# Start and end of a hybrid decoder layer: first weights by ScalarE's queue, one output block by ScalarE and an adding transfer, one load cut in two, one square moved

## The chip, the cores and the metric

The kernel runs on one core of one Trainium2 chip. The core has five engines that run beside each other, each with its own instruction queue in program order: TensorE (PE; its weight loads are PEld), VectorE (DVE), ScalarE (ACT), GpSimd (POOL) and SyncE (SP). SP, ACT and POOL can issue DMA transfers. The metric is the device time of one execution in microseconds (us), lower is better.

## The reference

One layer of a decoder trunk on 256 tokens, with 16 learned meta tokens ahead of them (L = 272), D = 2048, all in float32:

```
h = concat(meta, x)
u = rms_norm(h, g_pre_mix);  proj = u @ w_in
z_pool, v_conv, g_conv, gate_a, gate_b = split(proj)
y_a = causal_multiscale_pool(z_pool) @ w_pool_out
y_b = silu(layer_norm(depthwise_conv(v_conv * sigmoid(g_conv)))) @ w_conv_out
m = sigmoid(gate_a) * y_a + sigmoid(gate_b) * y_b
h = h + rms_norm(m @ w_o, g_post_mix)
f = square(relu(rms_norm(h, g_pre_mlp) @ w_up)) @ w_down
out = (h + rms_norm(f, g_post_mlp))[16:]
```

`rms_norm` divides each token's row by the root of the mean of its squares and multiplies by a gain per channel.

## The kernel before

**Exact products.** Each float32 operand is split into a high part (`hi`, a cast on ACT) and a low part (`lo = raw - hi`, a subtraction on DVE). A product is hi*hi + hi*lo + lo*hi, three matmuls (`mm3`) for each block of 128 channels. So every chunk of weights (1 MB, called `raw...`) passes through DMA, ACT (cast) and DVE (subtraction) before PE can use it.

**The first pass.** It computes 256 of the convolution's columns (`v_conv`) in two PSUM banks (`accs`, `acc_v`). Its weights are the chunks `raw_0` and `raw_1`, loaded in pieces. For each of the KD = 16 blocks of channels `x_tile(k)` turns the tokens (two PE transposes into `xt_k`) and splits them, with the gain `g_pre_mix`, into the high and low part of `u`; `pieces_to(k + 1)` splits the weights' piece; `mm3` then multiplies. The meta tokens come in by `meta_tiles` and four `meta_parts`. Token loads (`load_x`) stand between the weights' pieces in SP's queue (`X_BEHIND`). `keep_warm` issues transposes that nobody reads.

**The token norm comes late.** The factor 1/rms of a token is not applied to `u`. `sq_tile` squares and sums the tokens on ACT: eight squares of 128 x 512 for `x` and four of 16 x 512 for the meta tokens. Those for `x` whose turn comes within the first pass are issued there, on odd k from `SQUARES_FROM` = 5 on; `squares_left` puts all others into the plan (below). Behind the last square come `mean` (DVE, `tot`), `root` (ACT, `rs_q_in`) and `newton` (DVE: five small steps to `r_in`, then three diagonal tiles `v`). `rows_step` then multiplies the diagonals with ones on PE (L898), which spreads the factor over all partitions in bank `y0`; DVE copies it to `rb`, and every bank of the first passes is scaled by `rb` when DVE empties it.

**The second pass on.** The second pass's first megabyte is `raw_2` (chunk number `FIRST` = 2), split in four pieces that the first pass's last steps issue. Then come `raw_s0a` (two chunks), `raw_p0`, `raw_p1`, `raw_p2` and so on. From here the order is made by a plan: steps are listed with an engine, a cost, reads and writes (`plan.add`), PE's order is as listed, and `Plan.order` simulates the engines. An engine that becomes free in that simulation takes, among the steps that are ready by then, the one that is due first (L148), even if a more urgent one is about to become ready. The order found is issued as it stands; on the chip every engine keeps it and waits on semaphores.

**The end.** A second plan covers the last product. The output has two halves of 128 tokens (t = 0 and 1) and four column blocks of 512. `finish_down(t, cuts)` computes block by block on DVE `dst * r + h` (L2187; `norm3.r` is the last norm's factor, the `raw{rooms_h[t]}` rooms hold h, loaded from `kept` in DRAM) and issues the output's transfer. `half_done` handles the two last halves of a block for t = 1; the second one makes `r1`.

Of the kernel before, what the change touches and what calls it, by code (L numbers as in the profile page):

```python
# [12 lines left out]
AF = mybir.ActivationFunctionType  # L13
ALU = mybir.AluOpType
PSUM = bass.MemoryType.PSUM

P = 128
CK = 4
CW = 512
# [13 lines left out]
SQUARES_FROM = 5  # L33
# [177 lines left out]
def hybrid_block(ctx: ExitStack, tc: tile.TileContext, ins: dict, out: bass.AP):  # L211
    nc = tc.nc
    x = ins["x"][0]
    meta = ins["meta"]
    T, D = x.shape
    M = meta.shape[0]
    L = M + T
    NT = T // P
    KD = D // P
# [26 lines left out]
    def f32(ap):  # L246
        return ap.bitcast(F32)

    def acc_tile(name):
        return psA.tile([P, CW], F32, tag="acc", name=name)  # L250
# [44 lines left out]
    NB = D // CW  # L295
# [4 lines left out]
    FIRST = KD // HALF[0]  # L300
# [9 lines left out]
    opened = []  # L310
# [14 lines left out]
    def part_tile(tag, n):  # L325
        key = f"{tag}{n % 3}"
        room = ready.pop(key) if key in ready else part_room(key, f"{tag}_{n}")
        place = PLACES.get(n, (1, 1))[("hi", "lo").index(tag)]
        shift = (place - 1 - 3 * KEYS.index(key)) % 4 * LINE
        return room[:, shift:shift + CK * CW]  # L330

    def open_chunk():
        n, slot = at["n"], at["slot"]
        at["n"] += 1
        at["slot"] += 1
        if n >= UP:
            PLACES[slot] = (2, 1)
        src, (rows, width) = stream[n]
        raw = raws.tile([P, CK * CW], F32, tag="raw", name=f"raw_{n}")
        if n in spare:  # L340
            both = big.tile([P, 2, CK * CW], F32R, tag=spare[n], name=f"parts_{n}")
            hi, lo = both[:, 0, :], both[:, 1, :]
        else:
            hi, lo = part_tile("hi", slot), part_tile("lo", slot)
        raw, hi, lo = (t.rearrange("p (k c) -> p k c", k=rows) for t in (raw, hi, lo))
        pieces = rows if n < FIRST else 4 if n == FIRST else 1
        k = rows // pieces
        cuts = ((0, 1, 2, 4, 6, 8), (0, 2, 4, 6, 8))[n] if n < FIRST else (0, rows)
        for a_, b_ in zip(cuts, cuts[1:]):
            sl = slice(a_, b_)  # L350
            nc.sync.dma_start(raw[:, sl, :], src[:, sl, :])
            if (n, b_) in X_BEHIND:
                load_x(X_BEHIND[n, b_])

        def high(sl):
            nc.scalar.copy(hi[:, sl, :], raw[:, sl, :])

        def low(sl):
            nc.vector.tensor_sub(lo[:, sl, :], raw[:, sl, :], f32(hi[:, sl, :]))

        def piece(i):
            def f():
                sl = slice(i * k, (i + 1) * k)
                high(sl)
                low(sl)
            return f
        todo = [piece(i) for i in range(pieces)]
        if n in spare:
            todo = [lambda: high(slice(0, rows)), lambda: low(slice(0, rows))]
        opened.append((hi, lo, todo))  # L370
# [53 lines left out]
    def col(name, k):  # L424
        return vecs[:, cols[name] + k:cols[name] + k + 1]
# [4 lines left out]
    def load_x(b):  # L430
        sl = slice(b * X_COLS, (b + 1) * X_COLS)
        nc.sync.dma_start(x_in[:, :, sl], xv[:, :, sl])
# [20 lines left out]
    def keep_warm(n):  # L453
        for _ in range(n):
            nc.tensor.transpose(idle[:, :P], ident, ident)
# [30 lines left out]
    u = Tokens((K_FIRST, "um", 0), (KD - K_FIRST, "um8", 3 * LINE))  # L486

    def x_tile(k):
        pt = acc_tile(f"xt_{k}")
        sl = slice(k * P, (k + 1) * P)  # L490
        for t in range(NT):
            nc.tensor.transpose(pt[:, t * P:(t + 1) * P], x_in[:, t, sl], ident)
        at_ = slice(M, L)
        nc.scalar.activation(u[:, k, 0, at_], pt[:, :T], AF.Copy, scale=col("g_pre_mix", k))
        nc.vector.scalar_tensor_tensor(
            u[:, k, 1, at_], pt[:, :T], col("g_pre_mix", k), f32(u[:, k, 0, at_]),
            op0=ALU.mult, op1=ALU.subtract)
# [19 lines left out]
    def sq_tile(b, t):  # L517
        sl = slice(b * CW, (b + 1) * CW)
        junk = tmp.tile([P, CW], F32, tag="junk", bufs=1, name=f"sqx_{b}_{t}")
        src, n = (x_in[:, t, sl], P) if t < NT else (m_in[:, sl], M)  # L520
        nc.scalar.activation(junk[:n, :], src, AF.Square, accum_out=ssq[:n, t, b:b + 1])
# [12 lines left out]
    def mm3(acc, hi, lo, act, k, cs, first, last):  # L534


        off = act.shape[3] - acc.shape[1]
        for n, (w, a) in enumerate(((hi, 0), (hi, 1), (lo, 0))):
            nc.tensor.matmul(acc, w[:, k[0], cs], act[:, k[1], a, off:],  # L539
                             start=first and n == 0, stop=last and n == 2)  # L540
# [18 lines left out]
    def acc_tiles(name, n=CW // P):  # L559
        return [acc_tile(f"acc_{name}_{j}") for j in range(n)]  # L560
# [5 lines left out]
    def pieces_to(n):  # L566

        while first["split"] < min(n, FIRST * HALF[0]):
            c = first["split"] // HALF[0]
            opened[c][2].pop(0)()  # L570
            first["split"] += 1
# [4 lines left out]
    accs = [acc[:, :L] for acc in first_banks]  # L576
    squares = [(b, t) for b in range(XB) for t in range(NT)] + [(b, NT) for b in range(XB)]
    LEAD = 3
    TURNS = {0: (2, 3), 1: (), 2: (4, 5)}

    def turn_and_split(k):
        if k < KD:
            x_tile(k)
        pieces_to(k + 1)

    meta_parts.pop(0)()
    for k in range(2):
        turn_and_split(k)
    keep_warm(DUMMIES[1])
    for k in range(KD):  # L590
        for j, acc in enumerate(accs):
            mm3(acc, *opened[k // HALF[0]][:2], u, (k % HALF[0], k), slice(j * P, (j + 1) * P),
                k == 0, k == KD - 1)
        for n in TURNS.get(k, (k + LEAD,)):
            turn_and_split(n)
        if k < 3:
            meta_parts.pop(0)()
        if k >= SQUARES_FROM and k % 2 and k < KD - LEAD:
            sq_tile(*squares.pop(0))
        for _ in range((2, 1, 1)[k - KD + LEAD] if k >= KD - LEAD else 0):  # L600
            opened[FIRST][2].pop(0)()
# [13 lines left out]
    plan = LoadedPlan()  # L615
# [125 lines left out]
    n = 0  # L741
# [759 lines left out]
    norm3 = Norm("mlp")  # L1501
    ssq2 = const.tile([P, NT, NB], F32, name="ssq2")
    kept = dram.tile([P, NT, D], F32, name="kept")
# [155 lines left out]
    accs = acc_tiles("up00")  # L1659
# [51 lines left out]
    hi, lo = fetch()  # L1711
# [36 lines left out]
    ov = out[0].rearrange("(t p) d -> p t d", p=P)  # L1748

    plan = LoadedPlan()  # L1750
# [71 lines left out]
    def raw_in(room):  # L1822
        return room_of[room][:, :CK * CW]
# [289 lines left out]
    for j in range(4):  # L2113
        plan.add("PE", 1.36, last_of_first(j), reads=(f"hi{q0}", f"lo{q0}"),
                 writes=(f"x{j // 2}{j % 2}",))
    loads()
    for t in range(NT):
        plan.add("ACT", 0.92, lambda t=t: square_h1(t, NB - 1),
                 reads=[f"raw{r}" for r in H_ROOMS], writes=("junk", "ssq2"))
# [10 lines left out]
    for s, i in steps:  # L2130
        if s == "R":
            plan.add("PE", 0.9, rows2, reads=("diag2",), writes=("b",))
            plan.add("DVE", 0.4, lambda: nc.vector.tensor_copy(rb[:, :T], banks["b"][:, :T]),
                     reads=("b",), writes=("rb",))
# [39 lines left out]
    for t in range(NT):  # L2174
        add_bank(t, 2, f"x0{t}")
        for n in range(NB - 1):
# [2 lines left out]
        plan.add("DVE", 0.4, lambda t=t: norm3.start(t),  # L2179
                 reads=[f"ssq{t}{n}" for n in range(NB - 1)], writes=(f"v{t}",))  # L2180

    def finish_down(t, cuts, ahead=(), after=()):
        for n, (c0, c1) in enumerate(zip(cuts, cuts[1:])):
            dst = dst_of(t, c0, c1)

            def f(dst=dst, c0=c0, c1=c1, queue=(nc.sync, nc.scalar)[t * n % 2]):
                nc.vector.scalar_tensor_tensor(dst, dst, norm3.r[:, t],  # L2187
                                               raw_in(rooms_h[t])[:, c0:c1],
                                               op0=ALU.mult, op1=ALU.add)
                queue.dma_start(ov[:, t, c0:c1], dst)  # L2190
            plan.add("DVE", (c1 - c0 + 151) / 960 - 0.02, f,
                     reads=[f"out{t}{b}" for b in range(c0 // CW, (c1 - 1) // CW + 1)]
                     + [f"r{t}", f"raw{rooms_h[t]}", *after], writes=ahead)

    ends = [(m_, "X3"), (m_ + 1, "X4")]
    for w, s in ends:
        h = AT[s][0]
        plan.add("PE", 2.72, lambda w=w, h=h: down(banks["x10"], split_at[w], h, A1, False, h == 1),
                 reads=half_names(w) + act_names(h, A1), writes=("x10",), late=0.2)
    whole, name = total_of(0, NB - 1)  # L2200
    total = raw_in(room_s)[:, :CW]
    plan.add("DVE", 0.61, lambda: nc.vector.tensor_add(total, whole, banks["x10"]),
             reads=("x10", name), writes=(f"raw{room_s}",), late=0.1)
    plan.add("ACT", 0.92, lambda: square_of(total, norm3.ssq, 0, NB - 1), reads=(f"raw{room_s}",),
             writes=("junk", f"ssq0{NB - 1}"))
    plan.add("DVE", 0.69, lambda: nc.vector.tensor_mul(whole, total,
                                                       raw_in(room_g)[:, block(NB - 1)]),
             reads=(f"raw{room_s}", f"raw{room_g}"), writes=(f"out0{NB - 1}", name))
    plan.add("DVE", 1.3, lambda: norm3.finish(0), reads=("v0", f"ssq0{NB - 1}"), writes=("r0",))
    finish_down(0, (0, CW), ("first out",))  # L2210
    col_halves = [slice(h * HALF_CW, (h + 1) * HALF_CW) for h in range(2)]
    last_ssq = const.tile([P, 2], F32, name="last_ssq")
    for e, cs in enumerate(col_halves):
        for w, s in ends:
# [3 lines left out]
                reads=half_names(w) + act_names(h, A2), writes=("ab"[e],), late=0.2)  # L2218

        def half_done(e=e, cs=cs):  # L2220
# [9 lines left out]
            else:  # L2230
                for f in norm3.steps(1, last_ssq[:, 1:2]):
                    f()
        plan.add("DVE", (0.9, 2.3)[e], half_done,
                 reads=("ab"[e], "G3", "v1", ("first out", "next out")[e]),
                 writes=("junk", "v1", "G3", "out13") + (("r1",) if e else ()))
        if e == 0:
            finish_down(0, (CW, 2 * CW, 3 * CW), ("next out",))
    finish_down(0, (3 * CW, D), after=("r1",))
    finish_down(1, (0, 384, D // 2, D // 2 + CW, D - HALF_CW, D))
    plan.emit()  # L2240

# [24 lines left out]
```

## Time and profile before

| | us |
|---|---|
| median of 3 runs (lowest, highest) | 1180.18 (1179.68, 1180.21) |
| the profiled execution: its own time | 1180.13 |
| the profiled execution: span in the trace | 1178.3 |
| busy: PE, PEld | 1165.8, 1011.7 |
| busy: DVE, ACT, POOL | 1064.0, 707.3, 65.5 |

The trace's times count from the span's start. 1.83 us of the execution lie outside the span. Rows of a timeline give start, duration, engine, source line, operation, output and inputs, and in brackets the engine's idle time before the row with what ended it. "SPq" and "ACTq" are the queues' issue of a transfer. Matmuls are pipelined, so a row's duration is longer than the distance to the next.

### The profile page before, as it was taken

The page shows a single profiled execution, that of the slowest core. Times are in us where ns is not written, and L with a number is a line of the kernel's source. Part 1 is how long each engine was busy: PE and PEld are TensorE (multiplying, and loading weights), DVE is VectorE, ACT ScalarE, POOL GpSimd, SP SyncE. Part 2 cuts the span into 40 slices and gives each one's busy share as a digit, 9 for nine tenths or more (in the row PEclk, how much of TensorE's full clock was granted, in tenths as well). Part 3 has the DMA queues.
Part 4 walks back from the last instruction along what each step waited for, and adds up shares of the span by engine and source line. Part 5 has one row for each costly group of instructions (what it writes and reads, how often), then busy time and mean ns, then how long its engine had stood idle before and what let it go on. Part 6 is the DMA issues. An engine that isn't in the chain of part 4 may idle for free.

```text
span 1178.3 us, 15808 instructions
## 1 busy us (share of the span) xinstructions
PE 1165.8 (99%) x6301; PEld 1011.7 (86%) x6301; DVE 1064.0 (90%) x1156; ACT 707.3 (60%) x719; POOL 65.5 (6%) x68
## 2 busy tenths in 40 slices
PE   9999999999999999999999999999999999999996
PEld 8999998788888888898888888888888888888885
DVE  5899999999998998688998998998989989989857
ACT  6634455556478666575775666666656756656542
POOL 1000000000000000000101001000000010010000
PEclk9999999999999999999999999999999999999998
DMA  9955356789866799468999999999999999999941
GB/s 288 286 191 179 108 179 178 237 272 298 218 194 245 212 352 292 151 221 278 263 310 235 249 318 258 250 288 244 302 263 227 341 237 249 317 240 240 341 144 71
DMA packets 186977, 287.70 MB, mean 244 GB/s; under 512 B 4905, under 2 KB 94697, under 8 KB 186120
## 3 DMA queue, kind: packets, MB, share of 16 engines
q1 hardware_dynamic: 161960, 234.44, 58.2%
q0 software_dynamic: 24480, 51.67, 24.0%
q8 instruction: 49, 0.80, 0.3%
q10 hardware_dynamic: 464, 0.60, 0.1%
q14 instruction: 24, 0.20, 0.0%
HBM read 282.49 MB, written 4.19 MB: 243 GB/s over the span
## 4 chain that ended last, share of the span: by engine, by line
PE 95%; DMA 2%; DVE 2%; issue 0%; ACT 0%; DVEq 0%; POOL 0%; ACTq 0%; POOLq 0%
PE bank_u L544 18%; PE bank_k L1262 16%; PE acc_up L2005 13%; PE bank_u L550 9%; PE acc_v L1262 9%; PE bank_k L539 8%; PE bank_a L2005 7%; PE bank_b L2005 5%; PE acc_v L539 4%; PE acc_up L544 1%; DMA raw_k<-in_w_in_dram 1%; PE bank_u L2005 1%; DMA raw_p<-in_w_in_dram 1%; DVE lo L832 1%; PE acc_up L550 1%
## 5 line engine op out<-in xcount | busy, mean ns | idle before, releaser
L544 PE MATMUL bank_u<-m,hi 128*128 128x512 f32 x960 | 329.2, 389 | 0.0
L550 PE MATMUL bank_u<-m,lo 128*128 128x256 f32 x960 | 265.2, 276 | 0.0
L544 PEld LDWEIGHTS bank_u<-m,hi 128*128 128x128 f32 x960 | 180.2, 188 | 37.7
L826 ACT CAST hi<-raw_p 128x2048 fp32r<-128x2048 f32 x70 | 133.8, 1913 | 104.6 <-PE bank_k L1262 28.6
L1835 DVE TENSOR_TENSOR lo<-raw_m,hi 128x2048 fp32r<-128x2048 f32 x75 | 171.6, 2289 | 20.0 <-ACT hi L1830 18.8
L550 PEld LDWEIGHTS bank_u<-m,lo 128*128 128x128 f32 x960 | 180.2, 188 | 1.6
L1830 ACT CAST hi<-raw_m 128x2048 fp32r<-128x2048 f32 x75 | 143.5, 1913 | 60.3 <-PE bank_u L544 39.8
L832 DVE TENSOR_TENSOR lo<-raw_p,hi 128x2048 fp32r<-128x2048 f32 x70 | 159.6, 2283 | 12.6 <-ACT hi L826 12.4
L2005 PE MATMUL acc_up<-hi,forms 128*128 128x512 f32 x440 | 143.9, 390 | 0.0
L1835 DVE TENSOR_TENSOR lo<-raw_h,hi 128x2048 fp32r<-128x2048 f32 x43 | 98.3, 2287 | 11.1 <-ACT hi L1830 10.6
L1830 ACT CAST hi<-raw_h 128x2048 fp32r<-128x2048 f32 x43 | 82.2, 1911 | 41.6 <-PE bank_u L544 20.7
L962 DVE SCALAR_TENSOR_TENSOR c<-a,taps,c 128x256 f32<-128x256 f32 x240 | 99.9, 472 | 0.0
L2005 PEld LDWEIGHTS acc_up<-hi,forms 128*128 128x128 f32 x440 | 82.6, 188 | 18.0 <-ACT G L2030 0.2
L539 PE MATMUL bank_k<-u_um,hi 128*128 128x272 f32 x512 | 95.2, 287 | 0.0
L1262 PE MATMUL bank_k<-hi,u_um 128*128 128x512 f32 x280 | 88.8, 389 | 0.7 <-ACT sg L1311 0.7
L2005 PE MATMUL acc_up<-lo,forms 128*128 128x512 f32 x220 | 85.9, 391 | 0.0
L2005 PE MATMUL bank_a<-hi,forms 128*128 128x512 f32 (+1 forms) x256 | 81.9, 383 | 0.0
L539 PEld LDWEIGHTS bank_k<-u_um,hi 128*128 128x128 f32 x512 | 79.7, 188 | 0.0
L539 PE MATMUL bank_k<-u_um,lo 128*128 128x272 f32 x256 | 73.3, 287 | 0.0
L1830 ACT CAST hi<-raw_c 128x2048 fp32r<-128x2048 f32 x23 | 43.9, 1909 | 44.1 <-PE bank_u L544 36.7
L1835 DVE TENSOR_TENSOR lo<-raw_c,hi 128x2048 fp32r<-128x2048 f32 x23 | 52.6, 2286 | 13.2 <-ACT hi L1830 13.2
L2005 PE MATMUL bank_b<-hi,forms 128*128 128x512 f32 (+1 forms) x200 | 63.5, 381 | 0.0
(400 smaller groups left out, 2229.8 us busy)
## 6 DMA issues: line engine op xcount, KB each, us to landing
raw_p<-in_w_in_dram SPq DMA_DIRECT2D x30, 1024.0 KB, 5.3
raw_m<-in_w_down_dram SPq DMA_DIRECT2D x25, 1024.0 KB, 7.8
raw_m<-in_w_down_dram POOLq DMA_DIRECT2D x23, 1024.0 KB, 10.3
raw_h<-in_w_up_dram SPq DMA_DIRECT2D x20, 1024.0 KB, 7.5
raw_m<-in_w_up_dram SPq DMA_DIRECT2D x17, 1024.0 KB, 7.7
raw_h<-in_w_down_dram SPq DMA_DIRECT2D x17, 1024.0 KB, 8.8
raw_c<-in_w_down_dram SPq DMA_DIRECT2D x15, 1024.0 KB, 5.2
raw_k<-in_w_in_dram SPq DMA_DIRECT2D x14, 1024.0 KB, 7.8
```

Of the source, the lines that this page charges most:

```text
L539: nc.tensor.matmul(acc, w[:, k[0], cs], act[:, k[1], a, off:], start=first and n == 0, stop=last and n == 2)
L544: nc.tensor.matmul(acc.rearrange("p (a t) -> p a t", a=2)[:, :, ts], hi[:, k[0], cs], act[:, k[1], :, off + ts.start:off + ts.stop], start ...
L550: nc.tensor.matmul(acc[:, :T], lo[:, k[0], cs], act[:, k[1], 0, off:], start=False, stop=stop, skip_group_check=True)
L826: nc.scalar.copy(box["flat"][:, cs], rooms[q]()[:, cs])
L832: nc.vector.tensor_sub(lo[:, cs], rooms[q]()[:, cs], f32(box["flat"][:, cs]))
L962: nc.vector.scalar_tensor_tensor(C_c()[:, q, :], A_a()[:, q, i:i + T], taps[:, q, i:i + 1], C_c()[:, q, :], op0=ALU.mult, op1=ALU.add)
L1262: nc.tensor.matmul(banks[bank], a_(k, part), box[w_][:, k, :], start=opens and k == 0 and i == 0, stop=ends_ and k == CK - 1 and i == 2, s ...
L1830: nc.scalar.copy(box["flat"], raw_in(room))
L1835: nc.vector.tensor_sub(lo, raw_in(room), f32(box["flat"]))
L2005: nc.tensor.matmul(acc, forms[h][:, f, k, a_, :], box[w_][:, k, cs], start=start and k == 0 and n == 0, stop=stop and k == KH - 1 and n == ...
```

## The change

Seven edits, all at the two ends of the kernel:

- The first piece of `raw_0` (128 KB, channel block 0) is issued on ACT's queue behind the first tokens, not on SP's.
- `raw_2`, 1 MB, is loaded by two transfers of 512 KB.
- At the start, the weights' first piece is split ahead of the tokens' block 0 and the meta tokens' first part.
- Channel block 0 is multiplied in another order (`first_step`): both banks' hi*hi and lo*hi, then both banks' hi*lo.
- The transposes of tokens' block 4 stand between the two banks of block 2.
- The squares of the first pass end two steps earlier, so three stand there and not four. The fourth goes to `squares_left`.
- The last column block of t = 0 is no longer finished by DVE. ACT scales it by `r` into a free part of the room `raw_a` (512 columns), a transfer on POOL's queue adds the rows of `kept` from DRAM to it, and SP issues its output from there.

```diff
@@ open_chunk
-        cuts = ((0, 1, 2, 4, 6, 8), (0, 2, 4, 6, 8))[n] if n < FIRST else (0, rows)
+        cuts = {0: (0, 1, 2, 4, 6, 8), 1: (0, 2, 4, 6, 8), FIRST: (0, 4, 8)}.get(n, (0, rows))
         for a_, b_ in zip(cuts, cuts[1:]):
             sl = slice(a_, b_)
-            nc.sync.dma_start(raw[:, sl, :], src[:, sl, :])
+            queue = nc.scalar if (n, b_) == (0, 1) else nc.sync
+            queue.dma_start(raw[:, sl, :], src[:, sl, :])
@@ the first pass
-    TURNS = {0: (2, 3), 1: (), 2: (4, 5)}
...
+    pieces_to(1)
+    x_tile(0)
     meta_parts.pop(0)()
-    for k in range(2):
-        turn_and_split(k)
+    turn_and_split(1)
     keep_warm(DUMMIES[1])
+
+    def first_step():
+        hi, lo = opened[0][:2]
+        off = u.shape[3] - L
+        for terms in (((hi, 0), (lo, 0)), ((hi, 1),)):
+            for j, acc in enumerate(accs):
+                for w, a in terms:
+                    nc.tensor.matmul(acc, w[:, 0, j * P:(j + 1) * P], u[:, 0, a, off:],
+                                     start=w is hi and a == 0, stop=False)
+
     for k in range(KD):
-        for j, acc in enumerate(accs):
+        for j, acc in enumerate(accs if k else ()):
+            if k == 2 and j:
+                turn_and_split(LEAD + 1)
             mm3(acc, *opened[k // HALF[0]][:2], u, (k % HALF[0], k), slice(j * P, (j + 1) * P),
-                k == 0, k == KD - 1)
-        for n in TURNS.get(k, (k + LEAD,)):
+                False, k == KD - 1)
+        if k == 0:
+            first_step()
+        for n in (2, 3) if k == 0 else (k + LEAD,) if k > 1 else ():
             turn_and_split(n)
         if k < 3:
             meta_parts.pop(0)()
-        if k >= SQUARES_FROM and k % 2 and k < KD - LEAD:
+        if k >= SQUARES_FROM and k % 2 and k < KD - LEAD - 2:
             sq_tile(*squares.pop(0))
@@ the end
+    rest = raw_in(room_s)[:, CW:2 * CW]
+    rest_cols = slice((NB - 1) * CW, D)
+
+    def scale_and_add():
+        nc.scalar.activation(rest, whole, AF.Copy, scale=norm3.r[:, 0])
+        nc.gpsimd.dma_start(rest, kept[:, 0, rest_cols], accum_op=ALU.add)
+    plan.add("ACT", 0.58, scale_and_add, reads=("r0", f"out0{NB - 1}"), writes=("rest",))
...
-    finish_down(0, (3 * CW, D), after=("r1",))
+    plan.add("DVE", 0.01, lambda: nc.sync.dma_start(ov[:, 0, rest_cols], rest),
+             reads=("r1", "rest"), writes=("rest out",))
     finish_down(1, (0, 384, D // 2, D // 2 + CW, D - HALF_CW, D))
```

(`finish_down` also loses its argument `after`.) Lines of the changed kernel stand up to 23 lines further down: L898 is L913 there.

The plan makes its order anew. On PE, SP and POOL nothing moves beyond the edits themselves. On ACT and DVE it moves work around the token norm. ACT in the kernel before, from the last square of the tokens on (`sqx_3_1`; `sqx_b_t` is column block b of token half t, and t = 2 are the meta tokens; `rs_q_in` is the norm's root):

```order
L521 ACTIVATE sqx_3_1_503,ssq_124<-x_in_95 128x512
L826 CAST hi_5_505<-raw_p0_405 128x2048
L521 ACTIVATE sqx_0_2_534,ssq_124<-m_in_96 16x512
L521 ACTIVATE sqx_1_2_538,ssq_124<-m_in_96 16x512
L521 ACTIVATE sqx_2_2_564,ssq_124<-m_in_96 16x512
L521 ACTIVATE sqx_3_2_567,ssq_124<-m_in_96 16x512
L874 ACTIVATE rs_q_in_572<-tot0_569 128x3
L395 ACT_TABLE_LOAD
L395 ACTIVATE warm_93<-ones_91 128x1
L826 CAST hi_6_599<-raw_p1_406 128x2048
```

The same place on ACT in the changed kernel:

```order
L522 ACTIVATE sqx_3_0_502,ssq_125<-x_in_95 128x512
L841 CAST hi_5_504<-raw_p0_404 128x2048
L522 ACTIVATE sqx_3_1_533,ssq_125<-x_in_95 128x512
L522 ACTIVATE sqx_0_2_537,ssq_125<-m_in_96 16x512
L522 ACTIVATE sqx_1_2_563,ssq_125<-m_in_96 16x512
L522 ACTIVATE sqx_2_2_566,ssq_125<-m_in_96 16x512
L522 ACTIVATE sqx_3_2_568,ssq_125<-m_in_96 16x512
L841 CAST hi_6_597<-raw_p1_405 128x2048
L889 ACTIVATE rs_q_in_599<-tot0_594 128x3
L396 ACT_TABLE_LOAD
L396 ACTIVATE warm_93<-ones_91 128x1
L841 CAST hi_7_641<-raw_p2_406 128x2048
```

One more square stands behind the cast of `raw_p0`, and the cast of `raw_p1` has moved ahead of the norm's root.

DVE in the kernel before, from the subtraction of `raw_p0` to that of `raw_p1` (`tot0` is the mean, `r_in` the factor, `v_0` to `v_2` the diagonals that PE waits for):

```order
L832 TENSOR_TENSOR lo_5_536<-raw_p0_405,hi_5_505 128x2048
L869 TENSOR_REDUCE tot0_569<-ssq_124 128x3
L870 TENSOR_SCALAR tot0_569<-tot0_569 128x3
L525 RECIPROCAL r_in_601<-rs_q_in_572 128x3
L526 TENSOR_TENSOR rs_q_in_572<-r_in_601 128x3
L527 TENSOR_TENSOR rs_q_in_572<-rs_q_in_572,tot0_569 128x3
L528 TENSOR_SCALAR rs_q_in_572<-rs_q_in_572 128x3
L529 TENSOR_TENSOR r_in_601<-r_in_601,rs_q_in_572 128x3
L882 TENSOR_SCALAR v_0_408<-ident_86,r_in_601 128x128
L882 TENSOR_SCALAR v_1_409<-ident_86,r_in_601 128x128
L882 TENSOR_SCALAR v_2_410<-ident_86,r_in_601 16x16
L832 TENSOR_TENSOR lo_6_634<-raw_p1_406,hi_6_599 128x2048
```

The same place on DVE in the changed kernel:

```order
L847 TENSOR_TENSOR lo_5_535<-raw_p0_404,hi_5_504 128x2048
L884 TENSOR_REDUCE tot0_594<-ssq_125 128x3
L885 TENSOR_SCALAR tot0_594<-tot0_594 128x3
L847 TENSOR_TENSOR lo_6_602<-raw_p1_405,hi_6_597 128x2048
L526 RECIPROCAL r_in_628<-rs_q_in_599 128x3
L527 TENSOR_TENSOR rs_q_in_599<-r_in_628 128x3
L528 TENSOR_TENSOR rs_q_in_599<-rs_q_in_599,tot0_594 128x3
L529 TENSOR_SCALAR rs_q_in_599<-rs_q_in_599 128x3
L530 TENSOR_TENSOR r_in_628<-r_in_628,rs_q_in_599 128x3
L897 TENSOR_SCALAR v_0_407<-ident_86,r_in_628 128x128
L897 TENSOR_SCALAR v_1_408<-ident_86,r_in_628 128x128
L897 TENSOR_SCALAR v_2_409<-ident_86,r_in_628 16x16
```

The subtraction of `raw_p1` has moved from behind the diagonals to ahead of the factor's first step. PE's order is the same in both: the three products with the diagonals stand behind the second `raw_s0a` chunk and ahead of `raw_p0`.

More of the change, by code (lines that the diff above doesn't have):

```diff
@@ L2180, in hybrid_block, with finish_down @@
                  reads=[f"ssq{t}{n}" for n in range(NB - 1)], writes=(f"v{t}",))
-    def finish_down(t, cuts, ahead=(), after=()):
+    def finish_down(t, cuts, ahead=()):
         for n, (c0, c1) in enumerate(zip(cuts, cuts[1:])):
@@ L2192, in finish_down @@
                      reads=[f"out{t}{b}" for b in range(c0 // CW, (c1 - 1) // CW + 1)]
-                     + [f"r{t}", f"raw{rooms_h[t]}", *after], writes=ahead)
+                     + [f"r{t}", f"raw{rooms_h[t]}"], writes=ahead)
     ends = [(m_, "X3"), (m_ + 1, "X4")]
```

## The prediction

> **What bounds the kernel now.** I read the page's shares first, then the chain that ended last, then PE's waits, then the timelines of the stretches that the change touches. Shares of busy time and the chain's shares by engine, from the page:
>
> ```profile
> PE 1165.8 (99%) x6301; PEld 1011.7 (86%) x6301; DVE 1064.0 (90%) x1156; ACT 707.3 (60%) x719; POOL 65.5 (6%) x68
> PE 95%; DMA 2%; DVE 2%; issue 0%; ACT 0%; DVEq 0%; POOL 0%; ACTq 0%; POOLq 0%
> ```
>
> The waits of PE (engine, line and tile waited for: total, times, longest):
>
> ```profile
> PE idle L455 <- POOL ident masks.py:199: 1.4, 1, 1.4
> PE acc_v L1262 <- DVE lo L832: 0.7, 2, 0.5
> PE bank_k L1262 <- ACT sg L1311: 0.7, 1, 0.7
> ```
>
> PE is busy for 1165.8 of 1178.3 us and waits 2.8 us in three places, of which only 1.4 us come after the start. So PE is the bound nearly throughout: a microsecond that PE loses early in the kernel returns as a microsecond at the end, and only the ends, where something else bounds, have anything to give. What is early or late on ACT or DVE counts only where PE stands waiting for it.
>
> The change works at both ends, where that is so. But its moved square also makes the plan anew, and the rows shown with the change put the cast of `raw_p1` ahead of the norm's root, and its subtraction ahead of the norm's factor, while PE still takes the diagonals ahead of `raw_p0`. So the place to read is the norm, around 34 to 45 us.
>
> **The norm: how early the diagonals are now, and how late they get.** ACT's and DVE's timelines (start, duration), then PE's:
>
> ```profile
> 30.34 1.91 ACT L826 CAST hi<-raw_s0a 128x2048 fp32r<-128x2048 f32 x1 [0.56 <-DMA raw_s0a<-in_w_in_dram]
> 33.44 0.19 ACT L521 ACTIVATION_READ_ACCUMULATOR sqx<-x_in 128x1 f32 x1
> 34.19 0.18 ACT L521 ACTIVATION_READ_ACCUMULATOR sqx<-x_in 128x1 f32 x1
> 34.29 1.90 ACT L826 CAST hi<-raw_p 128x2048 fp32r<-128x2048 f32 x1
> 38.88 0.18 ACT L521 ACTIVATION_READ_ACCUMULATOR sqx<-m_in 16x1 f32 x1
> 39.57 0.20 ACT L874 ACTIVATE rs_q_in<-tot 128x3 f32<-128x3 f32 x1 [0.50 <-DVE tot L870]
> 41.19 3.70 ACT L826 CAST hi<-raw_p 128x2048 fp32r<-128x2048 f32 x2
> ```
>
> ```profile
> 36.21 2.29 DVE L832 TENSOR_TENSOR lo<-raw_p,hi 128x2048 fp32r<-128x2048 f32 x1 [1.20 <-ACT hi L826]
> 39.80 0.18 DVE L525 RECIPROCAL r_in<-rs_q_in 128x3 f32<-128x3 f32 x1 [0.27 <-ACT rs_q_in L874]
> 40.81 0.61 DVE L882 TENSOR_SCALAR v<-ident,r_in 128x128 f32<-128x128 f32 x3
> 43.11 2.29 DVE L832 TENSOR_TENSOR lo<-raw_p,hi 128x2048 fp32r<-128x2048 f32 x1 [1.69 <-ACT hi L826]
> 45.32 0.43 DVE L902 COPY rb<-bank_y 128x272 f32<-128x272 f32 x1
> ```
>
> ```profile
> 41.88 1.03 PE L898 MATMUL bank_y<-v,ones 16*128 16x16 f32 x6
> ```
>
> Before, the last diagonal is done at 40.81 + 0.61 = 41.42 and PE takes it at 41.88, without a wait: 0.46 us of room. PE's first of these products reads the diagonal of the meta tokens, which DVE makes last, so none of the six can go ahead of the whole chain.
>
> In the changed kernel, step by step, with these durations:
>
> 1. One more square of 128 x 512 on ACT behind the cast of `raw_p0`: the distance of two squares' ends is 34.19 − 33.44 = 0.75. The last square is read at 38.88 + 0.75 = 39.63.
> 2. The cast of `raw_p1` follows at once, 0.10 later (as 34.19 to 34.29): 39.73.
> 3. Its subtraction on DVE starts 1.92 later (34.29 to 36.21): 41.65. The mean is done in between, and the root's cost on ACT lies beside the subtraction.
> 4. The RECIPROCAL starts when the subtraction is through, 2.21 later (43.11 to 45.32): 43.86. Before it started at 39.80: the factor loses 4.06.
> 5. The last diagonal is done 1.62 later (39.80 to 41.42): 45.48, and PE starts some 0.05 behind: 45.53.
>
> Against 41.88 that is **+3.65** on PE: the factor's 4.06 less the room of 0.46, with the 0.05 of step 5. Nothing else of PE's own can fill the gap: `raw_p0` stands behind the products in its queue, and everything behind that.
>
> What can take from it: ACT's work from 30.34 on runs without a gap, and at 30.34 it waited for the landing of the second `raw_s0a` chunk. If the stream of loads is earlier, all of the above is. The first of the weights' two issues on SP leaves that queue:
>
> ```profile
> 2.05 0.90 SPq L351 DMA_DIRECT2D raw<-in_w_in_dram  x2
> 5.00:6.00 1.00, 1.00 (x7) 1.00 (x6) 0.54 (x2) 0.50 (x2) 0.00 (x0) 1.00 0.86 190
> 13.00:16.00 3.00, 3.00 (x27) 3.00 (x26) 2.34 (x7) 2.79 (x9) 0.00 (x0) 1.00 1.10 349
> ```
>
> (The last two are windows: the final columns are the granted clock, the DMA engines' share and GB/s.) One issue costs 0.90/2 = 0.45 us, and at 5 to 6 us the engines move 190 GB/s where they later move 349, so early issue is worth something there; from 13 us on the stream is full, and keeps what lead it has. I take 0.4, between 0 and 0.45. By "DMA: Bandwidth & Descriptors", Rules for kernel authors, in the Trainium skill, spreading transfers over engines saves issue time only; the unfilled window above is such a time, and with a lead of zero the sum would be 0.4 higher. **The gap: 3.65 − 0.4 = 3.25.** `raw_2` in two loads costs at most one more such issue, 0.45, in SP's queue and lands its first half earlier; it lies in the full stream, so I cost it at nothing, and its bound is the lead falling to zero.
>
> **The start.** From the chain that ended last (start, us, what):
>
> ```profile
> 6.58 1.32 PE acc_v L539 x6
> 8.34 1.96 PE acc_v L539 x12
> 10.74 0.75 PE acc_v L539 x6
> 11.71 1.00 PE acc_v L539 x6
> 20.68 2.51 PE acc_v L539 x18
> 29.91 12.04 PE bank_k L539 x96
> ```
>
> Six matmuls take 0.75 where nothing holds them. So 1.32 holds 0.57 of stall, 1.96 for twelve 0.46, 1.00 holds 0.25, and 2.51 for eighteen 0.26: 1.54 in all, which split first, `first_step` and the moved transposes aim at. I take 1.0 us that PE is earlier at 29.91 (bounds 0 and 1.5). But none of it reaches the end: the 96 matmuls from 29.91 then end 1.0 earlier, the diagonals don't, and PE's gap grows from 3.25 to 4.25. ACT's issue of a weights' piece (some 0.45) lies in ACT's idle time, before its first cast.
>
> **What the gap does to the clock.** At both ends PE's rate differs. PE's timeline at the start and end, and two windows:
>
> ```profile
> 1.36 2.82 PE L455 MATMUL idle<-ident 128*128 128x128 f32 x12 [1.36 <-POOL ident masks.py:199]
> 6.58 0.71 PE L539 MATMUL acc_v<-u_um,hi 128*128 128x272 f32 x2
> 7.36 0.41 PE L539 MATMUL acc_v<-u_um,hi 128*128 128x272 f32 x2
> 1168.34 0.28 PE L2005 MATMUL bank_b<-hi,forms 128*128 128x256 f32 x1
> 1170.50:1171.00 0.50, 0.00 (x0) 0.00 (x0) 0.43 (x3) 0.00 (x0) 0.00 (x0) 0.97 0.02 4
> 1171.00:1171.50 0.50, 0.00 (x0) 0.00 (x0) 0.50 (x2) 0.00 (x0) 0.00 (x0) 0.50 0.00 0
> ```
>
> The last matmul ends at 1168.62; the granted clock is 0.97 in 1170.5 to 1171.0 and 0.50 behind it, so it fell some 2.4 us after PE stopped. A gap of 4.25 us is longer than that, so I expect PE to restart at half rate. For how long, the start gives a bound: from 1.36 on PE is fed, the two matmuls at 6.58 still take 0.71, those at 7.36 take 0.41: slow for up to 6 us (the clock's column reads 1.00 at 5 to 6 us all the same, so there I go by the matmuls). Half rate for t costs t/2, so the price lies between 0 (the clock holds) and 3.0. No row shows a recovery from a short gap; I take the middle, **1.5**.
>
> By "TensorE: Matmul & The Clock Gate", Part 1, in the Trainium skill, the clock falls after an idle window of about 3.4 us. By the trace it came 2.4 us after the last matmul, which such windows on a fixed grid allow; by the rule a gap of 4.25 us may hold a whole window or not, and that is rival B.
>
> **The end.** DVE's and SP's timelines, and two groups of transfers (median us from issue to landing at the end):
>
> ```profile
> 1165.71 1.41 DVE L2187 SCALAR_TENSOR_TENSOR F_raw<-F_raw,r_mlp,raw_m 128x512 f32<-128x512 f32 x2
> 1171.03 0.74 DVE L2187 SCALAR_TENSOR_TENSOR G<-G,r_mlp,raw_m 128x512 f32<-128x512 f32 x1
> 1171.69 1.41 DVE L2187 SCALAR_TENSOR_TENSOR F_raw<-F_raw,r_mlp,raw_h 128x384 f32<-128x384 f32 x2
> 1172.33 0.33 SPq L2190 DMA_DIRECT2D out_dram<-F_raw  x1
> kept<-h POOLq DMA_DIRECT2D x2, 256.0 KB, 3.0
> raw_p<-in_w_in_dram POOLq DMA_DIRECT2D x6, 1024.0 KB, 9.3
> ```
>
> The row at 1171.03 is t = 0's last block, between `r1` and t = 1's output. Without it t = 1 starts 1171.69 − 1171.03 = **0.66** earlier, and its transfers follow. In its place ACT scales the block behind the first `r` (1165.71), about 0.7 us, where ACT is free, and POOL's adding transfer follows at about 1166.5. It moves 256 KB: 3.0 us by the plain row of that size, 9.3/4 = 2.3 by the adding one of 1 MB, 9.3 if its time is all latency. It is wanted at 1172.33 − 0.66 = 1171.67, 5.2 us after issue. By the two nearer prices it is there; by the farthest it isn't, and SP, which issues in order, would hold t = 1's outputs behind it (rival D).
>
> **The sum.** 3.25 + 1.5 − 0.66 = +4.1 on the profiled execution's own 1180.13: **1184.2**. That execution is within 0.05 of the runs' median, so no correction.
>
> **The rivals.**
> - **B, the clock holds.** Then 3.25 − 0.66 = +2.6: 1182.7. For it: PE works again after 4.25 us, and no row of the page shows a clock that falls in mid-kernel. Against: 2.4 us sufficed at the end.
> - **C, the other side: the diagonals come in time.** Were they ready before PE asks (about 40.9 when PE is 1.0 early), the start's 1.0 and the tail's 0.66 would stand: −1.7, 1178.5. It decides from the point at which ACT's chain is 4.6 us earlier (45.53 − 40.9). The one idle time ahead of that chain is 0.56 at 30.34, and even the whole of it leaves 4.0. The first squares would have to go much earlier, which the order does not show. Only a chip that runs the order otherwise brings it.
> - **D, the adding transfer is late**, by 0.66 or more: the tail's gain is lost, 3.25 + 1.5 = +4.75: 1184.9, and above that for each further microsecond.
> - **The issue on ACT's queue speeds nothing**: the lead is 0 and the gap 3.65, +4.5: 1184.6. It lies inside the forecast.
>
> **How the numbers follow.** About 0.2% (2.4 us) is what a measurement of this kernel can tell from no change. The forecast gets 0.68, B 0.16, D 0.09, C 0.07. The forecast's own ends: 3.2 + 0.5 − 0.66 = 3.0 with a short slow clock, 3.65 + 3.0 − 0.66 = 6.0 with the long one. The range goes from B's 2.6, less the lead's 0.05 and rounding, to 6.0 plus half of D's: 1182.4 to 1186.5. Slower by over 0.2% means above 1182.5: all of the forecast and D and two thirds of B, 0.68 + 0.09 + 0.11 = 0.88. Within 0.2%: the rest of B and half of C, 0.09. Faster: C with the whole 1.5 of the start and an earlier first matmul beside it, 0.03.
>
> **What would show it.** PE's waits should have a new row, the diagonals' products waiting some 4 us for DVE's `v`, with the RECIPROCAL near 43.5 and the subtraction of `raw_p1` right before it. The chain's first-pass matmuls should start earlier and PE's 96 matmuls end near 40.9. The windows at 44 to 50 us should show a granted clock of 0.5 in part. At the end `F_raw` of t = 1 should start right behind `r`. If PE shows no such wait, the reading of the order was wrong, and the time comes out near C.

## The result, and the profile after

| | us |
|---|---|
| before: median of 7 runs (lowest, highest) | 1179.68 (1178.79, 1180.48) |
| changed: median of 7 runs (lowest, highest) | 1183.07 (1182.36, 1183.93) |
| ratio, 95% interval | 1.003 (1.002 to 1.0039) |
| profiled execution of the changed kernel: own time, span | 1183.93, 1182.2 |

The change costs 3.4 us. The forecast was 1184.2, in a range from 1182.4 to 1186.5, slower: the sign, the place and the mechanism came as forecast, and the size was 1.1 us too large. (Against the 1180.18 of the table in the front the difference is 2.9; the seven runs of before lie around 1179.68.)

The waits of PE in the changed kernel:

```profile
PE bank_y L913 <- DVE v L897: 3.6, 1, 3.6
PE idle L456 <- POOL ident masks.py:199: 1.4, 1, 1.4
PE bank_k L1277 <- ACT sg L1326: 0.7, 1, 0.7
```

The first row is new: PE stands 3.6 us ahead of its products with the diagonals, for DVE's `v`. The chain to it, in the timelines of ACT, DVE and PE:

```profile
29.39 1.91 ACT L841 CAST hi<-raw_s0a 128x2048 fp32r<-128x2048 f32 x1 [0.42 <-DMA raw_s0a<-in_w_in_dram]
38.68 0.18 ACT L522 ACTIVATION_READ_ACCUMULATOR sqx<-m_in 16x1 f32 x1
38.77 1.89 ACT L841 CAST hi<-raw_p 128x2048 fp32r<-128x2048 f32 x1
40.57 0.20 ACT L889 ACTIVATE rs_q_in<-tot 128x3 f32<-128x3 f32 x1
40.70 2.29 DVE L847 TENSOR_TENSOR lo<-raw_p,hi 128x2048 fp32r<-128x2048 f32 x1 [1.36 <-ACT hi L841]
42.90 0.17 DVE L526 RECIPROCAL r_in<-rs_q_in 128x3 f32<-128x3 f32 x1
43.90 0.61 DVE L897 TENSOR_SCALAR v<-ident,r_in 128x128 f32<-128x128 f32 x3
40.70 0.29 PE L540 MATMUL bank_k<-u_um,lo 128*128 128x272 f32 x1
44.57 1.76 PE L913 MATMUL bank_y<-v,ones 16*128 16x16 f32 x6 [3.58 <-DVE v L897]
```

Every step is there: the last square, the cast of `raw_p1` 0.09 behind it, its subtraction, and only then the RECIPROCAL at 42.90, against 39.80 before. The root itself was ready at 40.8 and lay there for 2 us. PE's last matmul ahead of the gap ends at 40.99 and the products start at 44.57. They take 1.76 and not 1.03. The reason stands in the windows (PE busy in the second column, the granted clock in the third from the right) and in the chain that ended last:

```profile
43.00:44.00 1.00, 0.00 (x0) 0.00 (x0) 0.83 (x6) 1.00 (x1) 0.00 (x0) 0.91 1.10 350
44.00:45.00 1.00, 0.43 (x2) 0.43 (x2) 0.51 (x3) 0.07 (x1) 0.00 (x0) 0.50 1.05 327
50.00:51.00 1.00, 1.00 (x7) 1.00 (x7) 0.52 (x2) 0.43 (x1) 0.00 (x0) 0.68 0.06 16
51.00:52.00 1.00, 1.00 (x10) 1.00 (x9) 0.64 (x2) 0.00 (x0) 0.00 (x0) 1.00 0.54 104
46.32 7.96 PE bank_k L540 x48
```

A mean of 0.91 over 43 to 44 is 1.00 for 0.82 us and 0.50 for 0.18: the clock fell at 43.82. A mean of 0.68 over 50 to 51 puts its return at 50.64. It was low for 6.8 us, of which PE worked 6.1, and `raw_p0`'s 48 matmuls took 7.96 where they took 5.93 before.

This execution is the slowest of the seven, and most of the others paid less for the clock. Over the whole span the mean granted clock is 0.995 in it and in the next slowest run (1183.70), and 0.996 in the other five. An estimate from the traces: a mean of 0.996 (0.9955 to 0.9965) stands for 8.3 to 10.6 us at half clock; at the span's end, with PE's work done, the clock is low for 4.2 to 7.5 us in the twelve traces here; what is left is more than nothing and less than 6.8. So the median run was probably slow at the norm for some 3.4 us, as the square alone is below, and paid about 1.5 us for it, while the profiled execution paid 2.7.

PE's lead and lag against before, at the same matmuls: the products at 44.57 against 41.88 are 2.69 late. Of the next rows, from the chains of both kernels (before first, then after, in each pair), the second pair shows how the lag shrinks:

```profile
182.95 5.44 PE acc_v L1262 x24
188.38 5.44 PE acc_v L1277 x24
313.16 2.72 PE acc_v L1262 x12
317.35 2.72 PE acc_v L1277 x12
```

At 183 us the lag is 5.43: the gap's 2.69 and 2.74 for the slow clock. At 313 us it is 4.19: here before had waited twice for a subtraction, and the changed kernel does not. (The row of PE's waits in the prediction counts 0.7 us of idle time for the two; from start to start they cost 1.24.) The end-alone version below is the same program as before up to there, and its trace has no such wait, so those 1.24 us don't belong to the change.

The end, in the timelines of PE, ACT, POOL, DVE and SP, and the adding transfer's group (median us from issue to landing):

```profile
1172.79 0.28 PE L2020 MATMUL bank_b<-hi,forms 128*128 128x256 f32 x1
1170.16 0.72 ACT L2229 ACTIVATE raw_a<-G,r_mlp 128x512 f32<-128x512 f32 x1 [0.87 <-DVE r_mlp L1508]
1171.18 0.88 POOL L2230 DMA_DIRECT2D raw_a<-kept  x1 [86.08 <-ACT raw_a L2229]
1175.60 1.42 DVE L2202 SCALAR_TENSOR_TENSOR F_raw<-F_raw,r_mlp,raw_h 128x384 f32<-128x384 f32 x2
1175.65 0.33 SPq L2260 DMA_DIRECT2D out_dram<-raw_a  x1
1176.25 0.33 SPq L2205 DMA_DIRECT2D out_dram<-F_raw  x1
raw_a<-kept POOLq DMA_DIRECT2D x1, 256.0 KB, 4.5
```

From the last matmul's start to the first step on t = 1's output it is 1175.60 − 1172.79 = 2.81 us, against 1171.69 − 1168.34 = 3.35 before: 0.54 gained. The adding transfer took 4.5 us, SP issued the block's output when it had landed, at 1175.65, and was free 0.27 us before t = 1's first output was ready to go.

### The profile page after: what moved, and what is told of

The parts are those of the page before. It is cut to its first block, busy times and chain, and to the rows that moved or that the text cites. A ratio compares the mean times of both kernels' runs of the same rounds, so it can differ in the third digit from the quotient of the medians.

```text
span 1182.2 us, 15812 instructions
## 1 busy us (share of the span) xinstructions
PE 1167.5 (99%) x6301; PEld 1014.0 (86%) x6301; DVE 1064.0 (90%) x1155; ACT 708.2 (60%) x720; POOL 66.6 (6%) x69
## 3 DMA queue, kind: packets, MB, share of 16 engines
HBM read 282.75 MB, written 4.19 MB: 243 GB/s over the span
## 4 chain that ended last, share of the span: by engine, by line
PE 95%; DMA 2%; DVE 1%; ACT 1%; issue 0%; SPq 0%; DVEq 0%; ACTq 0%
PE bank_u L545 18%; PE bank_k L1277 18%; PE acc_up L2020 13%; PE acc_v L1277 10%; PE bank_u L551 9%; PE bank_k L540 7%; PE bank_a L2020 7%; PE bank_b L2020 5%; PE acc_v L540 3%; PE acc_up L545 1%; DMA raw_s0a<-in_w_in_dram 1%; PE bank_u L2020 1%; DMA x_in<-in_x_dram 1%; PE acc_up L551 1%; PE acc_v L1547 0%; PE bank_k L1547 0%
```

## The experiments

Theory: the moved square makes the plan put `raw_p1`'s cast ahead of the norm's root, and that costs a gap on PE and a slow clock behind it. Rivals: the edits of the start or the end cost the time; the extra square is the cost and not the cast; the gap alone is paid and not the clock.

**The square back** (the changed kernel, its squares as before):

```diff
-        if k >= SQUARES_FROM and k % 2 and k < KD - LEAD - 2:
+        if k >= SQUARES_FROM and k % 2 and k < KD - LEAD:
```

> The changed kernel with the squares of the first pass as before (four of them, the moved square undone). The order of ACT and DVE around the norm is again that of the kernel before. Theory (the wait comes from the order at the norm): PE takes the diagonals without a wait near 40.9 us, the clock stays at 1.00, and what is left are the start's 1.0 us and the end's 0.54: 1.5 under the kernel before, near 1178.2. Rival (the start's edits or the adding transfer cost the time): it stays near 1183.

Measured: 1178.15 (11 runs) against 1179.68, ratio 0.9988 (0.9979 to 0.9996). The diagonals and their products in its timeline and chain:

```profile
39.91 0.61 DVE L897 TENSOR_SCALAR v<-ident,r_in 128x128 f32<-128x128 f32 x3
41.46 0.96 PE bank_y L913 x6
42.42 5.93 PE bank_k L540 x48
```

No wait for the diagonals, no slow clock: the other six edits are worth about 1.5 us, and one moved square turns that into a loss of 3.4.

**The root first** (the changed kernel with its square still moved; `w == 4` is the split of `raw_p1`):

```diff
-                plan.add("ACT", 1.82, high, reads=names, writes=(h_,), late=0.13)
+                plan.add("ACT", 1.82, high, reads=names + ["root"] * (w == 4), writes=(h_,), late=0.13)
```

> The changed kernel with its square still moved, but the plan told that the cast of raw_p1 needs the norm's root: root, factor and diagonals go ahead of that cast and its subtraction again. Theory: the last square ends at 38.9 as in the changed kernel, the factor starts 0.9 later at 39.8, the last diagonal is done 1.62 later near 41.3, PE waits some 0.4 at most and keeps its clock: within 0.5 of the version with the square back, near 1178.6. Rival (the extra square behind the cast is itself the cost, not the cast ahead of the root): a wait of 1 us or more, 1180 or above.

Measured: 1178.01 (11 runs), ratio 0.9987 (0.9978 to 0.9996). The diagonals, and PE's part of the chain:

```profile
40.22 0.61 DVE L897 TENSOR_SCALAR v<-ident,r_in 128x128 f32<-128x128 f32 x3
41.51 0.96 PE bank_y L913 x6
42.47 5.93 PE bank_k L540 x48
```

The last diagonal is done at 40.22 + 0.61 = 40.83 and PE does not wait. So the extra square is not the cost, the cast ahead of the root is. This and the version above beat both kernels, and the two cannot be told apart.

**The square alone** (the kernel before with only the first version's line changed the other way):

> The kernel before with the moved square alone (three squares in the first pass); nothing else of the change. Theory: the order at the norm is that of the changed kernel, the loads have no lead: the diagonals come at 45.5, PE waits 3.65 us from 41.9, the clock falls to 0.5 for some 6 us (2.75 us of PE's time, as in the changed kernel), and 1.2 of the delay is taken up by a later wait: +5.2, near 1184.9, slower than the changed kernel. Rival (the other edits make the wait): no change from before, 1179.7.

Measured: 1184.12 (5 runs), ratio 1.0041 (1.0028 to 1.0054), the slowest of all. PE's wait, `raw_p0`'s matmuls in the chain, and two windows:

```profile
PE bank_y L898 <- DVE v L882: 2.9, 1, 2.9
45.86 7.45 PE bank_k L539 x48
45.00:46.00 1.00, 1.00 (x8) 0.97 (x8) 0.10 (x1) 0.00 (x0) 0.00 (x0) 0.83 1.09 347
49.00:50.00 1.00, 1.00 (x10) 1.00 (x9) 1.00 (x2) 0.00 (x0) 0.00 (x0) 0.96 0.23 78
```

By the same working the clock fell at 45.66 and came back at 49.08, 3.4 us later, half of the 6.8 in the changed kernel's trace. The gap is 2.9 and not 3.65, because in this execution the cast of the second `raw_s0a` chunk started at 29.61, not 30.34, though no load was edited.

**The end alone and the start alone** (the kernel before with the one group of edits each):

> The kernel before with the end's edits alone: ACT scales the last block of t = 0, the adding transfer adds the rows of h, SP issues the output. Theory: t = 1's output starts 0.6 to 0.7 us earlier after the last matmul, the adding transfer has landed by then: 0.65 under before, near 1179.0. Rival (the adding transfer is late or disturbs t = 1's output): before or above, 1179.7 or more. Up to 246 us this is the kernel before unchanged, so its trace also shows whether PE's wait for a subtraction at 242 us comes back.

> The kernel before with the start's edits alone (first weights on ACT's queue, raw_2 in two loads, the weights' first piece split first, the first block's other order, block 4's transposes between the banks), the squares as before and the end as before. Theory: the order at the norm is that of before, PE is 0.5 to 1.0 us earlier there and stays so: near 1178.9. Rival (the early stream is given back at later waits): before, 1179.7.

Measured: the end 1178.88 (11 runs, 0.9999, 0.999 to 1.0008), the start 1178.94 (11 runs, 0.9996, 0.9987 to 1.0005), against 1179.35. Medians 0.5 and 0.4 lower; neither interval excludes no change, only both together show one (the square back). The traces are clearer on the end: in the end-alone version the first step on t = 1's output stands 1170.37 − 1167.56 = 2.81 us behind the last matmul's start, as in the changed kernel. In the start-alone version PE starts the products with the diagonals at 41.32, 0.56 us ahead of before (41.88) and 0.89 ahead of the end-alone version (42.21), whose start is that of before: two executions of the same start differ by 0.33 there.

**The gap filled** with transposes that nobody reads, in the changed kernel, 30, 20 or 12:

```diff
+            for _ in range(30):
+                nc.tensor.transpose(banks["y0"][:, CW - P:], ident, ident)
             for t, lo_, n in [(NT, 0, M)] + [(t, M + t * P, P) for t in range(NT)]:
```

> The changed kernel with 30 transposes of the identity, which nobody reads, on PE ahead of the products with the diagonals (0.11 us each, 3.3 us, so they end before the diagonals come at 44.6). The order of the other engines is unchanged. Theory (the gap costs its length and, apart from that, a slow clock): the products still start near 44.6, but the clock stays at 1.00 and raw_p0's 48 matmuls take 5.93 and not 7.96: 2.75 less than the changed kernel, near 1180.3. Rival (the price is the wait alone, the clock's fall hidden): 1183, as the changed kernel.

> The changed kernel with 20 such transposes, 2.3 us of the gap filled, 1.3 left: no step with less than 60% busy. Theory: no fall of the clock; raw_p0's 48 matmuls take 5.9; if the waits for loads near 216 and 242 us that the version with 30 showed were its run's own, 1180.4 to 1181; if the loads set the pace there whenever PE comes less late, 1182 to 1183 with a wait for sg over 1 us again.

> The changed kernel with 12 transposes of the identity, unread, on PE ahead of the products with the diagonals: 1.4 us of the gap filled, some 2.2 left. The clock moved in steps of 3.41 us in the traces so far, and fell after a step with PE busy for 17, 25 and 31% of it, while 78% did not bring it back. Theory (a step's busy share decides): a gap of 2.2 leaves at least 36% busy, so the fall comes seldom or not; where it does, PE's row shows 7 us or more for raw_p0's 48 matmuls. With no fall the time is 1.5 to 2.7 under the changed kernel, 1180.4 to 1181.6. Rival (only a step with no work at all brings the fall): never a fall, the same time. Rival (the price is paid later all the same, as in the version with 30 transposes): near 1182.8.

Measured: 1182.78 (11 runs), 1181.84 (7) and 1182.31 (7), ratios 1.0027 (1.0018 to 1.0036), and 1.0025 (1.0014 to 1.0036) twice. The products in PE's timelines with 30, 20 and 12, and `raw_p0`'s matmuls in the chains:

```profile
45.32 1.03 PE L915 MATMUL bank_y<-v,ones 16*128 16x16 f32 x6 [0.71 <-DVE v L897]
46.35 5.93 PE bank_k L540 x48
```

```profile
44.42 1.03 PE L915 MATMUL bank_y<-v,ones 16*128 16x16 f32 x6 [1.33 <-DVE v L897]
45.45 5.92 PE bank_k L540 x48
```

```profile
44.11 1.03 PE L915 MATMUL bank_y<-v,ones 16*128 16x16 f32 x6 [1.84 <-DVE v L897]
45.14 5.93 PE bank_k L540 x48
```

The clock holds in all three traces: products 1.03, matmuls 5.93. Yet against their befores (1179.68, 1179.35 and 1179.35) they are still 3.1, 2.5 and 3.0 us slower, only 0.3 to 0.9 less than the changed kernel's 3.4: with 30 the time is the rival's, with 12 it lies 0.7 above the range expected. Part of the answer is that the changed kernel's median run paid about 1.5 for the clock and not 2.7, by the estimate above. (One run of each of the three has a mean clock of 0.996, so by the same estimate the clock fell there too; the traces are of other runs.) Two more things stood against the gain. With 30 the products started at 45.3, as that execution's loads were later (the cast of `raw_s0a` at 30.14). And in all three a later load came late: with 30 the second `raw_k` chunk, for which ACT's cast waited 2.05 us, with 20 and 12 the first, with waits of 1.33 and 1.38. ACT's casts of the first `raw_k` chunk behind 210 us, in the changed kernel and in the version with 12:

```profile
215.62 1.92 ACT L841 CAST hi<-raw_k 128x2048 fp32r<-128x2048 f32 x1 [0.28 <-PE acc_v L1277]
```

```profile
213.54 1.91 ACT L841 CAST hi<-raw_k 128x2048 fp32r<-128x2048 f32 x1 [1.38 <-DMA raw_k<-in_w_in_dram]
```

One waits for PE, the other 1.38 us for the load. The queues of the version with 12 in that stretch, 207 to 214 us (packets, MB, share of 16 engines):

```profile
q1 hardware_dynamic: 1001, 2.01, 77.1%
q0 software_dynamic: 177, 0.33, 25.9%
q8 instruction: 1, 0.02, 0.9%
q14 instruction: 1, 0.01, 0.3%
```

A fetch of instructions (the row of q8), one packet of 16 KB, took 0.9% of 16 engines over 7 us, which is 1.0 us of one engine, while the two rows of loads kept the engines busy (77.1 and 25.9%); in the changed kernel no row of a fetch stands in the same stretch. PE's program is 12 transposes longer, so that a fetch of it would come at another moment. Two more runs tested that.

**The same length** (the version with 12, the 12 transposes of `keep_warm` at PE's start left out):

```diff
-DUMMIES = (12, 3)
+DUMMIES = (0, 3)
```

> The version with 12 unread transposes in the gap, with the 12 unread transposes at PE's start left out, so that PE's program is as long from the norm on as in the changed kernel. In the three versions with transposes added, a 16 KB fetch of instructions (about 1.0 us on one of the 16 DMA engines) stood at 2 to 4 us into the load of a raw_k that is issued when PE frees its room (206.97 with 12), and the cast behind it started 1.1 us late; in the changed kernel it stands 6.9 us after that issue, behind the landing. Theory (the fetch's place costs 1.1 us): the fetch is back behind the landing, the cast of raw_k waits 0.4 or less for PE, not 1.4 for the load, and the time is some 1 us under the version with 12: 1181.0 to 1181.5. Rival (the loads set the pace whenever PE comes less late): the cast waits 1.4 us for the load again, near 1182.3.

**Longer without a gap** (the version with the root first, with 20 transposes at that place):

> The version with the root ahead of the cast (no gap at the norm), with 20 unread transposes ahead of the products: 2.3 us of PE's time and 20 instructions more. Theory (the fetch's place): the fetch stands within the raw_k load again, the cast behind it waits 1 us or more for the load, PE waits longer near 216 and 242 us: 2.3 + 0.8, near 1181.1. Rival (the late load belongs to the gap or to the order at the norm): no such wait, the 2.3 us of the transposes alone or less, 1180.3 or under.

Measured: 1180.66 (11 runs, 1.0012, 1.0003 to 1.0021) and 1181.28 (11 runs, 1.0014, 1.0006 to 1.0023), against 1179.25. The same cast of `raw_k`, first with the same length, then longer without a gap:

```profile
212.39 1.92 ACT L841 CAST hi<-raw_k 128x2048 fp32r<-128x2048 f32 x1 [0.21 <-PE acc_v L1279]
```

```profile
212.56 1.91 ACT L841 CAST hi<-raw_k 128x2048 fp32r<-128x2048 f32 x1 [1.40 <-DMA raw_k<-in_w_in_dram]
```

With the length restored the wait for the load is gone; with the gap gone and the transposes kept it is there. The place of the fetch in each trace, against this load (us):

| | load issued | fetch starts | issue to landing |
|---|---|---|---|
| changed kernel | 210.17 | 217.09 | 5.1 |
| root first | 204.29 | 211.24 | 5.2 |
| 12, same length | 206.94 | 213.85 | 5.4 |
| 30 transposes | 208.17 | 208.60 | 5.6 |
| 20 transposes | 207.26 | 209.04 | 6.4 |
| 12 transposes | 206.97 | 210.82 | 6.5 |
| root first, 20 | 206.04 | 207.88 | 6.4 |

With the fetch behind the landing the load takes 5.1 to 5.4, with the fetch 1.8 to 3.9 us into it 6.4 or 6.5. The version with 30, which the expectation above counts with the latter, is not one of them: its fetch started 0.43 us behind the issue, this load was hardly late, and why the next one was late is open. For the other three the wait goes with the length of PE's program and not with the gap. It reached PE: with 12 transposes and with 12 of the same length PE is 0.03 us apart at 60 us and 1.05 at 260.

The version of the same length came out below what was expected of it. It also bears on the slow clock: it still has the late diagonals (products at 44.09 in its chain, its slower start lies within the gap), but `raw_p0` takes 5.93. It is 1.4 us slower than its before, where the changed kernel is 3.4. That difference of 2.0 agrees with about 1.5 for the clock in a median run and the 0.48 by which its products start earlier (44.57 − 44.09).

## Why the prediction was right, step by step

- **PE is the bound, and a lag stays.** Held: the 5.43 us of lag stand unchanged from the norm to 183 us. What took some back was a wait in before's own execution.
- **The chain at the norm.** Each step came at its forecast distance. The RECIPROCAL was 2.20 behind the subtraction's start (2.21 forecast), the last diagonal 1.61 behind that (1.62), the products 0.06 later (0.05). The gap's cause is shown by the root put first, which takes it away with everything else left.
- **The lead of the loads was mis-sized**: 0.95 in the trace, where 0.4 was taken and 0.45 held for the most. With it the gap's 3.65 − 0.95 = 2.70 agrees with the measured 2.69. The fault was to price the landing by the one issue that leaves SP's queue. The landing varies by more than that between executions: the cast of the second `raw_s0a` chunk started at 30.34, 29.61 and 30.27 without the start's edits, and from 28.91 to 30.14 with them. The means of these three and nine traces are 0.7 apart. One trace of before cannot give that lead, and how much of it the edits bring is left open.
- **The start is swallowed.** Held: PE is 0.97 earlier at the end of the 96 matmuls (40.99 against 41.67 + 0.29 = 41.96) for 1.0 forecast, and waits that much longer. In the traces of the square back, the root first and the start alone, where nothing swallows it, PE is only 0.49, 0.45 and 0.56 ahead of before at the products.
- **The slow clock.** It fell, so rival B is out. The price was 2.74 in the changed kernel's trace, 1.5 with the square alone (7.45 − 5.93), for 1.5 forecast between 0 and 3. By the mean clocks above the median run paid about 1.5 too. That the forecast's middle fits it is luck: no row gave it, and the price comes in steps (below), of which the profiled execution paid two. One argument was also wrong. A window of 3.4 us without any work cannot end 2.4 us after the last matmul, as the prediction allows; so the end of before already spoke against an idle window as the condition.
- **The end.** 0.54 in the trace for 0.66. The removed row was 0.66 long, but t = 1's first step now stands where that row stood, directly behind its factor's last step, and starts 0.20 behind the start of that step, where the removed row had started 0.08 behind it: 0.12 less gain.
- **Rival D stood nearer than its price said.** The adding transfer took 4.5 us where 2.3 to 3.0 was the nearer estimate, and 0.27 us of room were left of the forecast 2.2 or more.
- **The sum.** In the two traces: 2.69 + 2.74 − 1.24 − 0.54 = 3.65; the spans differ by 3.9. The remaining 0.25 came between 600 and 650 us, and its cause is open. From the forecast's 4.1 one comes to the 3.9 by −0.55 (lead), +1.24 (clock), +0.12 (end), −1.24 (before's own wait) and the +0.25. The two largest misses cancel, so that the total came this near is in part luck; the mechanism did not depend on it. Over the runs the difference is 3.4, as the profiled executions lie above their medians, the changed kernel's by 0.86 and before's by 0.45. The forecast range's lower end is 0.3 below what its own terms give (1182.7); the measured 1183.07 lies inside either way.

## What to carry to other kernels

When a change touches anything that a scheduler orders, read the new order before pricing the edits: here one moved square of 0.75 us cost more than everything else brought. A step that is about to become ready loses to one that is ready, and a long cast ahead of a short root is paid on PE twice, in the gap and in the clock behind it; one more entry in a step's reads set it right, near 1178.0. And a probe that adds instructions moves the fetches too, so keep the program's length when a microsecond matters.

## What the hardware showed that was not expected

**The clock moves in steps of 3.41 us, and a step need not be empty to bring the fall.** The slow stretches were 6.82 us (43.82 to 50.64) and 3.42 us (45.66 to 49.08): two steps and one. In the step ahead of the fall PE had worked 0.59 of 3.41 us in the changed kernel (40.40 to 43.82), 0.86 with the square alone (44.80 to 45.66), and 1.06 at the end of before (1167.56 to 1168.62): 17, 25 and 31%. From 43.82 to 47.23 PE worked from 44.57 on, 78%, and the clock stayed low for another step. Gaps of 0.7, 1.3 and 1.8 us, which leave at least 46% of any step, brought no fall in these traces. The grid of steps holds through a whole trace: in the changed kernel the clock fell again at 1177.04 (its mean is 0.77 from 1176.50 to 1177.50), 1126.40 us or 330 steps after its return. Carried back from the falls at the end, the grid gives the least busy step that brought no fall: 56%, from 40.35 to 43.76 with 12 transposes. Where between 31 and 56% the border lies, no run shows. The Trainium skill's page "TensorE: Matmul & The Clock Gate", Part 1, has windows of 3413 ns that run freely, which these lengths bear out; it gives an idle window for the fall, and here 2.9 us without work sufficed at the norm and 2.35 us within a step at the end of before.

**A fetch of instructions takes a load's time.** One packet of 16 KB took 0.97 to 1.02 us in the three loads that it fell into, on one of the 16 DMA engines by its share above, and in these three traces the 1 MB load landed 6.4 or 6.5 us after its issue and not 5.1 to 5.4. ACT's cast then waited 1.3 to 1.4 us for the load, and in the version with 12 PE lost 1.0 us by it.
